# A quarter of the S5 turn tables moves from GpSimd to VectorE in a two-layer hybrid trunk

## The chip, the cores and the metric

The kernel runs as one program on one core of a Trainium2 chip. The metric is device microseconds for one execution. Engines are named as the profile names them: PE (TensorE), DVE (VectorE), ACT (ScalarE), POOL (GpSimd), and SP, whose queue issues most DMAs.

## The reference, cut to what matters

Two layers with the same structure work on 1024 tokens of width 1024 in fp32. Each layer normalises its input, projects it once, runs three branches on parts of the projection, and projects the concatenated result back:

```python
mod = silu(c) @ w_mod + b_mod                       # shift, scale, gate
h = rmsnorm(x, g_pre) * (1 + scale) + shift
a_q, a_k, a_v, a_g, b_q, b_k, b_v, b_lr, b_g, c_u, c_g = split(h @ w_in)
o_a = sliding_window_attention(a_q, a_k, a_v, sinks) * silu(a_g)
o_b = rmsnorm(gated_linear_attention(b_q, b_k, b_v, log_a), g_gla) * silu(b_g)
y = gelu(s5_ssm(c_u, a_re, a_im, log_dt, b_re, b_im, c_re, c_im, d))
o_c = y * sigmoid(y @ w_glu + b_glu) * silu(c_g)
x = x + gate * rmsnorm(concat(o_a, o_b, o_c) @ w_out, g_post)
```

The change lies in `s5_ssm`. It is a complex diagonal recurrence per state, h[t] = abar * h[t-1] + in[t], with abar = mag * (cos th + i sin th). The kernel takes 8 tokens as one step and turns the state's axes by the angle, so that the scan over 128 steps needs only the real factor rho = mag^8. For that it needs, for each of 32 groups of 64 states, the cosine and the sine of n times the angle of one step, for n from 0 to 127: the turn tables. They depend on the weights alone and are computed in the kernel, once per layer.

## The kernel before

**Stages of a layer.** The projection's products are split into a high and a low fp32r part: each weight tile is loaded by SP into `wraw` (3 buffers), cast by ACT to `whi` (L52) and subtracted on DVE to `wlo` (L53), 4 buffers each; PE then makes three matmuls for each product (L387 to L389, or L408 to L410 where the tokens are the output's rows). A queue of generators yields units of such projections, and other work is put between the units. A layer runs: the tail of the layer before; the values of the linear attention (`bv`, two projections) and its queries and keys (`bqk`, four) with the S5 tables between them; the linear attention (`gla`) with the S5 inputs (`cu`) and gates between; attention with the S5 scans between; the output projection.

**The table stage.** `s5_tables(l)` is a generator. It loads weights, forms `bf` and `cx`, and then runs two kinds of sub-generators for four parts q = 0 to 3: `blocks(q)`, which forms the tables E and O on DVE (`powmul`, L1179 to L1181), transposes E on PE into G and stores O and G to DRAM (L1170), and `turns(q)`, the turn tables. Part q starts two rounds after part q - 1. At the end come R (L1255, L1262) from the product `pk` of PE, and DMAs of R from SP (L1268, L1270). `gla_decay(l)` is put ahead of the rest of the tables after 10 units in layer 0, and after 18 in layer 1, where the tables have been issued in full by then. It transposes `lr` (L759, L760), multiplies (L768, L769, L770), takes Exp and Ln on ACT (L773, L774) and finishes the log decay on DVE (L778).

**The turn tables.** `turns(q)` works on 4 groups on each half of the partitions: tiles `cs` and `sn` of 128x4x128 and `rt` (a scratch), each with one buffer. It sets column 0 to 1 and 0 (L1217, L1218) and doubles the table seven times: with n = 1, 2, ..., 64 columns known, six products and sums of 128x4xn elements (L1225 to L1230) give the next n. Then the negated sine goes to the scratch (L1234), and three DMAs, issued from POOL's queue (L1235, L1237), store the sine's negative, the cosine and the sine to `s5turn` in DRAM. `s5_scan` reads them in the attention stage of the same layer (L1316), on SP's queue.

**After the stage.** `gla` clears `xq` on POOL (L694) and runs the scans `bc` on DVE (L786). POOL (L799), ACT (L800) and DVE (L804) then form the keys that PE transposes (L810).

**What sets the order.** The source is not the order on an engine. When the kernel is built, the framework sorts each engine's instructions by time estimates of its own: of those that it takes for ready, the one that stands earlier in the source goes first. A tile with one buffer is taken for ready when its last reader, a DMA included, is done by the estimate. On the chip each engine then works its list in order and waits on semaphores. (DVE's memset of `dc`, L1257, from the end of `s5_tables`, stands ahead of its first product, L1144, in the trace.)

Of the kernel before, what the change touches and what calls it, by code (L numbers as in the profile page):

```python
# [19 lines left out]
ALU = mybir.AluOpType  # L20
# [21 lines left out]
class Trunk:  # L42
# [1077 lines left out]
    def s5_tables(self, l):  # L1120
        nc = self.nc
        v, g_ = nc.vector, nc.gpsimd
# [88 lines left out]

        def turns(q):
            gs = slice(q * 4, q * 4 + 4)
            cs = st.tile([P, 4, P], F32, name="cs", bufs=1)
            sn = st.tile([P, 4, P], F32, name="sn", bufs=1)
            t3 = st.tile([P, 2, 4, 64], F32, name="rt", bufs=1)
            g_.memset(cs[:, :, 0:1], 1.0)  # L1217
            g_.memset(sn[:, :, 0:1], 0.0)  # L1218
            for k in range(7):
                n = 1 << k  # L1220
                zc = tcs[:, 0, k, gs].unsqueeze(2).to_broadcast([P, 4, n])
                zs = tcs[:, 1, k, gs].unsqueeze(2).to_broadcast([P, 4, n])
                a, b = t3[:, 0, :, 0:n], t3[:, 1, :, 0:n]
                lo, hi = slice(0, n), slice(n, 2 * n)
                g_.tensor_tensor(out=a, in0=sn[:, :, lo], in1=zs, op=ALU.mult)  # L1225
                g_.tensor_tensor(out=b, in0=cs[:, :, lo], in1=zs, op=ALU.mult)
                g_.tensor_tensor(out=cs[:, :, hi], in0=cs[:, :, lo], in1=zc, op=ALU.mult)
                g_.tensor_tensor(out=sn[:, :, hi], in0=sn[:, :, lo], in1=zc, op=ALU.mult)
                g_.tensor_tensor(out=cs[:, :, hi], in0=cs[:, :, hi], in1=a, op=ALU.subtract)
                g_.tensor_tensor(out=sn[:, :, hi], in0=sn[:, :, hi], in1=b, op=ALU.add)  # L1230
                if k > 3:
                    yield
            neg = t3.rearrange("p a g n -> p (a g n)").rearrange("p (g n) -> p g n", n=P)
            g_.tensor_scalar(out=neg, in0=sn, scalar1=-1.0, scalar2=1.0, op0=ALU.mult, op1=ALU.mult)  # L1234
            g_.dma_start(self.turn[l][:, 2, 4 * q:4 * q + 4, :], neg)  # L1235
            for slot, t in enumerate((cs, sn)):
                g_.dma_start(self.turn[l][:, slot, 4 * q:4 * q + 4, :], t)  # L1237

        flight = []
        for q in range(6):  # L1240
            if q < 4:
                flight.append(blocks(q))
                flight.append(turns(q))
            live = list(flight)
            for _ in range(2):
                for f in live:
                    if next(f, "end") != "end":
                        yield
                    elif f in flight:
                        flight.remove(f)  # L1250
        for f in flight:
# [9 lines left out]
                        in1=dc.unsqueeze(2).to_broadcast([P, 32, 16]), op=ALU.mult)  # L1261
# [352 lines left out]
```

## Time and profile before

| what | value |
|---|---|
| time, median of 3 runs | 1859.58 us (1851.38, 1859.58, 1863.3) |
| profiled execution | 1855.12 us, span 1853.3 us |
| PE busy | 1745.6 us (94% of the span) |
| DVE busy | 1342.5 us (72%) |
| ACT busy | 860.1 us (46%) |
| POOL busy | 586.2 us (32%) |
| mean granted PE clock | 0.979 of full speed |

The span runs from the first to the last instruction; the execution's own time lies 1.8 us above it. Busy shares are averages over stages with different limits; matmul ends are modelled, so a busy PE is not PE at its peak. Times in the rows below are microseconds from the span's start. A row's number in square brackets is the idle time of the engine just before it, with what ended it.

### The profile page before, as it was taken

The numbers are of one execution on the slowest core, as the hardware profiler recorded it, in microseconds if no ns is written. First come the engines' busy times: TensorE is split into PE (matmuls) and PEld (weight loads), VectorE is DVE, ScalarE is ACT, GpSimd is POOL, SyncE is SP. The second block draws the span as 40 slices with busy tenths as digits, with TensorE's granted clock in tenths as the row PEclk, the third lists the DMA queues.
The fourth block names the chain that finished last, engine by engine and source line by source line (L and its number), as shares of the span: only waits on it lengthen the run. The fifth ranks groups of instructions, "written<-read, shape, count | busy, mean of one in ns | idle before, by whom it ended". The sixth has DMA issues, their size and how long they took to land.

```text
span 1853.3 us, 28268 instructions
## 1 busy us (share of the span) xinstructions
PE 1745.6 (94%) x9403; PEld 1457.4 (79%) x9403; DVE 1342.5 (72%) x2975; ACT 860.1 (46%) x1973; POOL 586.2 (32%) x1005
## 2 busy tenths in 40 slices
PE   6999799999989989999998989999999899999998
PEld 5987588887777677788768968888888767878876
DVE  7876778479999788647675654974898978873534
ACT  5233333445556565446563243333555656642433
POOL 4269742212343354002116971411323511000100
PEclk8999899999999999999999999999999999999999
DMA  8144411235542322235464432212345111113342
GB/s 309 31 92 142 131 52 47 63 112 174 170 142 70 113 81 75 92 125 182 161 194 113 150 116 65 57 35 69 107 128 148 52 46 41 37 51 133 106 167 100
DMA packets 239385, 198.24 MB, mean 107 GB/s; under 512 B 49596, under 2 KB 195068, under 8 KB 239240
## 3 DMA queue, kind: packets, MB, share of 16 engines
q1 hardware_dynamic: 211640, 172.54, 31.0%
q10 hardware_dynamic: 25536, 16.80, 2.9%
q0 software_dynamic: 2064, 7.11, 1.0%
q8 instruction: 74, 1.21, 0.3%
q14 instruction: 71, 0.58, 0.1%
HBM read 163.13 MB, written 37.46 MB: 108 GB/s over the span
## 4 chain that ended last, share of the span: by engine, by line
PE 45%; DVE 9%; ACT 3%; issue 2%; DMA 2%; POOL 2%; ACTq 0%; DVEq 0%; POOLq 0%; SPq 0%
PE py L1486 15%; PE pj L387 5%; PE pj L389 5%; PE pj L388 5%; PE pj L1486 2%; PE pa L898 1%; PE pj L408 1%; PE pj L410 1%; PE pj L409 1%; DVE wlo L53 1%; PE pT L610 1%; PE pj L1384 1%; DVE pl L53 1%; DMA wraw<-in_w_out_dram 1%; DVE p L595 1%
## 5 line engine op out<-in xcount | busy, mean ns | idle before, releaser
L387 PE MATMUL pj<-H,whi 128*128 128x512 f32 x1088 | 442.8, 407 | 7.0 <-ACT M L665 3.2
L389 PE MATMUL pj<-H,wlo 128*128 128x512 f32 x1088 | 431.5, 397 | 3.2 <-DVE wlo L53 3.2
L388 PE MATMUL pj<-H,whi 128*128 128x512 f32 x1088 | 430.6, 396 | 0.0
L53 DVE TENSOR_TENSOR wlo<-wraw,whi 128x512 fp32r<-128x512 f32 (+1 forms) x320 | 237.1, 759 | 96.0 <-ACT whi L52 87.1
L52 ACT CAST whi<-wraw 128x512 fp32r<-128x512 f32 (+1 forms) x320 | 191.7, 618 | 179.2 <-PE pj L388 108.5
L387 PEld LDWEIGHTS pj<-H,whi 128*128 128x128 f32 x1088 | 207.4, 191 | 51.4 <-ACT M L665 3.6
L389 PEld LDWEIGHTS pj<-H,wlo 128*128 128x128 f32 x1088 | 206.6, 190 | 50.9 <-DVE wlo L53 4.2
L388 PEld LDWEIGHTS pj<-H,whi 128*128 128x128 f32 x1088 | 207.4, 191 | 39.9 <-issue 1.0
L600 ACT ACTIVATE p<-p,st 128x257 f32<-128x257 f32 (+1 forms) x256 | 125.7, 493 | 152.6 <-DVE st L595 138.7
L53 DVE TENSOR_TENSOR mlo<-M,mhi 128x384 fp32r<-128x384 f32 (+2 forms) x80 | 53.5, 676 | 141.6 <-ACT mhi L52 134.8
L1486 PE MATMUL py<-whi,mhi 128*128 128x512 f32 x448 | 142.6, 397 | 5.8 <-ACT mhi L52 3.1
L1486 PE MATMUL py<-wlo,mhi 128*128 128x512 f32 x448 | 145.1, 397 | 0.6 <-DVE wlo L53 0.5
L1486 PE MATMUL py<-whi,mlo 128*128 128x512 f32 x448 | 143.4, 394 | 0.7 <-DVE mlo L53 0.7
L1507 POOL TENSOR_SCALAR yrs<-yss 128x1 f32<-128x1 f32 x16 | 6.7, 418 | 376.0 <-ACT junk L1503 374.9
L52 ACT CAST mhi<-M 128x384 fp32r<-128x384 f32 (+2 forms) x80 | 50.3, 634 | 157.7 <-PE pj L1486 94.7
L595 DVE CUSTOM_DVE_ANT_0 p<-sc,bias,sink 128x256 f32<-128x256 f32 (+1 forms) x256 | 111.4, 462 | 5.7 <-PE sc L590 4.6
L1486 PEld LDWEIGHTS py<-whi,mhi 128*128 128x128 f32 x448 | 83.3, 188 | 27.6 <-ACT whi L52 5.3
L584 POOL COPY p<-sink 128x2 f32<-128x2 f32 x128 | 34.3, 270 | 221.2 <-PE pT L610 101.2
L1486 PEld LDWEIGHTS py<-wlo,mhi 128*128 128x128 f32 x448 | 84.4, 188 | 22.6 <-DVE wlo L53 3.7
L1486 PEld LDWEIGHTS py<-whi,mlo 128*128 128x128 f32 x448 | 84.4, 189 | 19.9 <-DVE mlo L53 1.5
L410 PE MATMUL pj<-wlo,H 128*128 128x256 f32 (+1 forms) x320 | 92.3, 291 | 6.2 <-DVE wlo L53 6.2
L408 PE MATMUL pj<-whi,H 128*128 128x256 f32 (+1 forms) x320 | 93.2, 292 | 3.8 <-DVE hv L346 2.7
(379 smaller groups left out, 3921.2 us busy)
## 6 DMA issues: line engine op xcount, KB each, us to landing
wraw<-in_w_in_dram SPq DMA_DIRECT2D x160, 256.0 KB
wraw<-in_w_out_dram SPq DMA_DIRECT2D x160, 256.0 KB
wraw<-in_w_mod_dram SPq DMA_DIRECT2D x64, 256.0 KB
M<-s5tab SPq DMA_DIRECT2D x32, 256.0 KB
M<-s5turn SPq DMA_DIRECT2D x64, 128.0 KB
M<-in_w_mod_dram SPq DMA_DIRECT2D x10, 512.0 KB
s5tab<-O ACTq DMA_DIRECT2D x8, 512.0 KB
s5tab<-G ACTq DMA_DIRECT2D x8, 512.0 KB
```

What stands on the lines that cost most here:

```text
L52: self.nc.scalar.copy(hi, src)
L53: self.nc.vector.tensor_tensor(out=lo, in0=src, in1=hi.bitcast(F32), op=ALU.subtract)
L387: nc.tensor.matmul(pj, hi, hh, start=(k == 0), stop=False)
L388: nc.tensor.matmul(pj, hi, hl, start=False, stop=False)
L389: nc.tensor.matmul(pj, lo, hh, start=False, stop=(k == KD - 1))
L408: nc.tensor.matmul(pj[:, :N], hh, hi, start=(k == 0), stop=False)
L409: nc.tensor.matmul(pj[:, :N], hl, hi, start=False, stop=False)
L410: nc.tensor.matmul(pj[:, :N], hh, lo, start=False, stop=(k == KD - 1))
L584: nc.gpsimd.tensor_copy(p[:, :, n], self.sink[:, h0:h0 + 2])
L595: nc.vector.tensor_tensor_reduce(out=p[:, h, 0:n], in0=sc[:, h * 256:h * 256 + n], in1=bias[:, h, o0:o0 + n], scale=-1.0, scalar=self.sink ...
L600: nc.scalar.activation(p[:, h, 0:n + 1], p[:, h, 0:n + 1], AF.Exp, bias=neg[:, h:h + 1], scale=-1.0, accum_out=den[:, h:h + 1])
L1486: self.nc.tensor.matmul(py[t, h], lhs, ws[h][w][:, 0, :], start=(n == 0 and first), stop=(n == N - 1 and last))
```

## The change

`turns(q)` takes its memsets, its 42 products and sums and the negation on DVE where q is 3, in both layers. The three DMAs stay on POOL's queue. The tiles and their single buffers are the same.

```diff
         def turns(q):
             gs = slice(q * 4, q * 4 + 4)
+            e_ = v if q == 3 else g_
             cs = st.tile([P, 4, P], F32, name="cs", bufs=1)
             sn = st.tile([P, 4, P], F32, name="sn", bufs=1)
             t3 = st.tile([P, 2, 4, 64], F32, name="rt", bufs=1)
-            g_.memset(cs[:, :, 0:1], 1.0)
-            g_.memset(sn[:, :, 0:1], 0.0)
+            e_.memset(cs[:, :, 0:1], 1.0)
+            e_.memset(sn[:, :, 0:1], 0.0)
             for k in range(7):
...
-                g_.tensor_tensor(out=a, in0=sn[:, :, lo], in1=zs, op=ALU.mult)
...
+                e_.tensor_tensor(out=a, in0=sn[:, :, lo], in1=zs, op=ALU.mult)
...
-            g_.tensor_scalar(out=neg, in0=sn, scalar1=-1.0, scalar2=1.0, op0=ALU.mult, op1=ALU.mult)
+            e_.tensor_scalar(out=neg, in0=sn, scalar1=-1.0, scalar2=1.0, op0=ALU.mult, op1=ALU.mult)
             g_.dma_start(self.turn[l][:, 2, 4 * q:4 * q + 4, :], neg)
```

The other five products and sums of a step change in the same way.

## Rows read from the trace of the kernel before

**Rows 1.** Waits, 198 to 220 us: waiter, awaited, us in total, times, longest.
```profile
PE pk L810 <- DVE M L804: 11.7, 1, 11.7
```

**Rows 2.** Waits, 1083 to 1100 us.
```profile
PE pj L387 <- ACT M L665: 3.2, 1, 3.2
```

**Rows 3.** Timeline of DVE in layer 0: start, us, instruction.
```profile
199.24 8.19 DVE L53 TENSOR_TENSOR wlo<-wraw,whi 128x512 fp32r<-128x512 f32 x2 [7.39 <-ACT whi L52]
207.36 6.80 DVE L786 TENSOR_TENSOR_SCAN bc<-ones,M 128x128 f32<-128x128 f32 x16
```

**Rows 4.** Timeline of DVE in layer 1.
```profile
1045.21 1.52 DVE L1181 TENSOR_TENSOR O<-O,pm_t 128x1024 f32<-128x1024 f32 x1
1056.58 0.69 DVE L1255 COPY R<-pk 128x512 f32<-128x512 f32 x1 [9.85 <-PE pk L1198]
...
1060.77 2.31 DVE L53 TENSOR_TENSOR wlo<-wraw,whi 128x512 fp32r<-128x512 f32 x3 [2.73 <-ACT whi L52]
1065.57 1.28 DVE L760 COPY M<-plr 16x512 f32<-16x512 f32 x2 [2.49 <-PE plr L759]
...
1083.03 5.82 DVE L778 SCALAR_TENSOR_TENSOR M<-M 128x512 f32<-128x512 f32 x1 [5.70 <-ACT M L774]
...
1091.76 6.80 DVE L786 TENSOR_TENSOR_SCAN bc<-ones,M 128x128 f32<-128x128 f32 x16
```

**Rows 5.** Timeline of POOL in layer 0.
```profile
194.32 0.20 POOL L1225 TENSOR_TENSOR rt<-sn,tcs 128x4 f32<-128x4 f32 x1 [1.28 <-DMA s5turn<-rt]
...
207.42 0.54 POOL L1235 DMA_DIRECT2D s5turn<-rt  x1
```

**Rows 6.** Timeline of POOL in layer 1.
```profile
986.56 0.10 POOL L1217 MEMSET cs<- 128x4 f32 x1 [7.86 <-PE pj L339]
...
1010.89 9.07 POOL L1226 TENSOR_TENSOR rt<-cs,tcs 128x16 f32<-128x16 f32 x1
...
1052.55 0.10 POOL L1217 MEMSET cs<- 128x4 f32 x1 [2.27 <-DMA s5turn<-cs]
...
1072.56 0.10 POOL L1217 MEMSET cs<- 128x4 f32 x1 [2.10 <-DMA s5turn<-cs]
...
1075.49 0.70 POOL L1225 TENSOR_TENSOR rt<-sn,tcs 128x4 f32<-128x4 f32 x1 [0.79 <-DMA s5turn<-rt]
...
1087.55 0.76 POOL L1230 TENSOR_TENSOR sn<-sn,rt 128x256 f32<-128x256 f32 x1
```

**Rows 7.** Timeline of ACT in layer 0.
```profile
201.35 0.62 ACT L52 CAST whi<-wraw 128x512 fp32r<-128x512 f32 x1 [2.14 <-PE pj L388]
```

**Rows 8.** DVE: timeline at 105 us; then a group by shape (count, busy, mean ns).
```profile
105.73 0.22 DVE L1086 TENSOR_TENSOR pa__1200<-M 128x64 f32<-128x64 f32 x1
105.88 0.22 DVE L1087 TENSOR_TENSOR pb__1201<-M 128x64 f32<-128x64 f32 x1
...
L1331 DVE TENSOR_TENSOR s5a<-s5a 128x256 f32<-128x256 f32 x32 | 13.4, 418 | 4.7 <-POOL s5a L1330 3.8
```

**Rows 9.** Timelines of ACT and POOL in one gelu step of layer 1.
```profile
1466.58 0.60 ACT L52 CAST whi<-wraw 128x512 fp32r<-128x512 f32 x1
...
1467.96 0.59 ACT L473 ACTIVATE qs<-pj 64x512 fp32r<-64x512 f32 x1
1469.34 0.63 ACT L1365 ACTIVATE ge<-ge 128x512 f32<-128x512 f32 x1 [0.79 <-POOL ge L1364]
...
1467.52 1.78 POOL L1364 TENSOR_TENSOR ge<-ge,M 128x512 f32<-128x512 f32 x1
```

**Rows 10.** Timeline of PE in layer 1.
```profile
1062.62 0.39 PE L389 MATMUL pj<-H,wlo 128*128 128x512 f32 x1
...
1068.66 0.69 PE L768 MATMUL pz<-M,wa 16*128 16x512 f32 x1
```

**Rows 11.** View of the tile rt: its DMAs from issue to landing.
```profile
DMA to landing us min/median/max: 2.5/4.3/5.5
```

**Rows 12.** Windows in layer 0: length, busy us by engine, PE clock, DMA share, GB/s.
```profile
218.00:222.00 4.00, 3.84 (x13) 3.43 (x14) 3.96 (x3) 2.25 (x4) 4.00 (x3) 0.50 0.02 5
```

More of the change, by code (lines that the diff above doesn't have):

```diff
@@ L1224, in turns @@
                 lo, hi = slice(0, n), slice(n, 2 * n)
-                g_.tensor_tensor(out=a, in0=sn[:, :, lo], in1=zs, op=ALU.mult)
[L1226 to L1230, printed above, removed]
+                e_.tensor_tensor(out=a, in0=sn[:, :, lo], in1=zs, op=ALU.mult)
+                e_.tensor_tensor(out=b, in0=cs[:, :, lo], in1=zs, op=ALU.mult)
+                e_.tensor_tensor(out=cs[:, :, hi], in0=cs[:, :, lo], in1=zc, op=ALU.mult)
+                e_.tensor_tensor(out=sn[:, :, hi], in0=sn[:, :, lo], in1=zc, op=ALU.mult)
+                e_.tensor_tensor(out=cs[:, :, hi], in0=cs[:, :, hi], in1=a, op=ALU.subtract)
+                e_.tensor_tensor(out=sn[:, :, hi], in0=sn[:, :, hi], in1=b, op=ALU.add)
                 if k > 3:
```

## The prediction

> **What bounds the kernel now.** I read the page's first part, then the waits of TensorE (PE), then the timelines of VectorE (DVE) and GpSimd (POOL) over the two stages in which the turn tables are made. PE is busy nearly all the time, so an edit on DVE or POOL is worth only what PE waits for it. In layer 0 PE makes no matmul for 11.7 us before L810, whose input comes from DVE L804 [rows 1]; in layer 1 it stands 3.2 us for a PSUM tile that ACT L665 frees late [rows 2]. Both waits end a chain that starts with the scans bc (L786).
>
> In layer 0 bc starts at 207.36, behind two weight splits (L53) that took 8.19 us together [rows 3]; R, an operation of the same width, takes 0.69, so two of them should take 1.4 [rows 4]. The same microsecond is the end of POOL's turn tables: their last DMA issue is at 207.42 [rows 5]. In layer 1 one L778 took 5.82 us, until 1088.85 [rows 4]; POOL's last table product starts at 1087.55 and lasts 0.76 [rows 6]. So DVE stood still while POOL ran products back to back. It goes the other way too: one POOL product of 128x16 elements took 9.07 us [rows 6] while DVE worked without a gap. The reader should keep both: POOL's last table holds up DVE on the chain that PE waits for, and DVE makes POOL's second table late.
>
> **The part that leaves POOL.** Per layer POOL loses 2 memsets, 42 products and the negation. Its own time is no term: the tables are read only in the attention stage. The credit is the end of DVE's stall. Layer 0: the second split's input comes at 201.97 [rows 7], so bc could start at 202.6 instead of 207.36, 4.8 us earlier. Layer 1: 5.82 less 0.7 is 5.1 us on the chain to L665, of which PE can use its wait of 3.2.
>
> At this credit the rows and the notes differ. L778 waited through nine POOL products, none over 0.76 us long near its end [rows 4, 6]. The Trainium skill (SBUF — State Buffer, section "SBUF: two separate sides") says that a DVE instruction with two SBUF inputs and a GpSimd one that reads SBUF take turns under an exclusive lock, held for the whole of one instruction. Read as a wait for one instruction, that gives L778 a credit of 0.8 us at most, and the sum below would end about 2 us higher. The trace shows the loser waiting for many, so I keep 5.1.
>
> **The part that DVE gains.** 45 instructions per layer. The 30 products up to 128x64 and the two memsets: DVE starts one of 128x64 0.15 us after the one before and is busy 0.22 [rows 8], so 32 of them take 4.8 to 7.0 us. Six of 128x128, between 0.22 and 0.42, take 1.3 to 2.5; six of 128x256 at 0.42 take 2.5 [rows 8]; the negation 0.7, as R [rows 4]. Sum 9.3 to 12.7 us; I take 9.5, since successive instructions overlap in the rows. It would be hidden where DVE is idle: 9.9 us before R at 1056.58, and 5.7 before L778 [rows 4].
>
> **The wait that the change adds.** cs, sn and rt have one buffer each. DVE's first memset must therefore wait until POOL has finished the third table and its DMAs have landed. In layer 1 POOL itself waited for them until 1072.56 (cs) and 1075.49 (rt) [rows 6]. DVE works in order, so everything queued behind that memset waits too. What is queued there is decided when the kernel is built: among the instructions that it takes for ready, the planner picks the one earlier in the source. The trace of before can't show where it puts the new ones, but it shows how it reckons POOL. In the gelu step it gave ACT four other instructions, from 1466.58 to 1468.55, between the square and the tanh, and then let the tanh wait 0.79 us for POOL's two operations [rows 9]. So it charges POOL about what POOL needs undisturbed, or less, and no stall. Undisturbed, the third table took 17.9 us: from 1052.55 to 1072.56, less the wait of 2.10 [rows 6]. Starting at 986.56 [rows 6], three of them end at about 1041, and the planner has the buffers free at about 1043. On the chip DVE slowed the second table, and the buffers come 30 us later. By the planner's reckoning the fourth table thus fits into DVE's idle stretch between the last O (ends 1046.4) and R (1056.58) [rows 4], and I expect it there in the order.
>
> **What that costs in layer 1.** Behind the table stand R, its sum, and the three splits of 1060.77 [rows 4], which give the weights of the first projection after the values. PE uses their lower halves from 1062.62 on [rows 10], so nothing covers a delay. The late end of the wait is 1075.5. The early end: POOL loses less to R, the splits and L760 (some 1.8 us, an estimate), and the landing of rt takes 2.5 us, the shortest, instead of 5.5, the longest [rows 11]: 1070.7. Half a microsecond of the table goes ahead of rt, 9.0 us follow: it ends between 1079.7 and 1084.5. R and its sum (1.4) and a split (0.7) come next, so PE gets its weights between 1081.8 and 1086.6, 19.2 to 24.0 us late. I take 19.2, the early end, because SP's loads stand behind R's DMAs and the queues are then quiet. After 11.7 us without work PE ran at half the clock in layer 0 (0.50 of full speed, the lower of the levels 1.2 and 2.4 GHz, from 218 to 222 [rows 12]); those 4 us hold work for 2, so I add 2 us. Against it, the chain to L665 moves by 21.2 less 5.1, and PE by 21.2, so PE no longer waits the 3.2. Layer 1: 19.2 + 2 - 3.2 = +18. Who else waits: R's eight DMAs on SP, with three weight loads behind them, wanted a projection later (some 11 us of PE's work hides them; without that they cost about 5), and the table's three DMA issues on POOL, now waiting for DVE, with the clearing of xq and L799 behind them. Those aren't wanted before bc, so they cost nothing; with DVE later than bc they would add their own 2 us each.
>
> **Layer 0.** The same wait would run to 194.3, when rt is free [rows 5], and the table to about 203. Splits stand further ahead of PE there, and a late one costs it between nothing and 12 us (203 against about 191, when the projection then due has used up its first half; an estimate). PE would meet its wait at L810 that much later, and that wait shrinks by up to 5. So the ends are -4.8 (bc at 202.6) and +7. I take 0, near the middle, as no row is nearer to either.
>
> **Sum.** The profiled execution took 1855.1 us, 1.8 beyond its span, and 4.5 below the median of the three runs (1859.6, from 1851.4 to 1863.3). With +18 and 0 it would take 1873; from the median, which I forecast, 1878. A change under 1% (18.6 us) can hardly be told from none in this kernel, and the forecast stands at that border.
>
> **Rivals.** A, not slower: the planner charges POOL 25 us or more per table. Then it has the buffers free only after about 1063; the table stands behind the splits and most of the decay (L760, L770) and runs in the gaps from 1072.6 on; L778 loses its stall, PE its wait. Layer 0 gives -3 (the table ends near 204, bc follows), layer 1 -3.2: 1853. For it: what holds up L778 and layer 0's bc is just the work that leaves. Against it: the gelu rows. It decides at the point where the memset stands behind L760 in DVE's order. B, between: the table stands behind the splits but ahead of L760 (1065.57 [rows 4]) or L770. PE then waits at L768 (1068.66 [rows 10]), which needs L760's output, for up to 16 us, or for some 6 if only L770 is late: +4 to +16, 1870 in the middle. C, earlier: the planner charges less than 17.9, and the table stands ahead of the last O and E (O's product starts at 1045.21 [rows 4]), so that the transposes of block 3 wait too, some 10 us of PE's work earlier (an estimate): +28, 1888. In any of them the new order may also move work elsewhere. That the change doesn't do what it says is excluded by the diff.
>
> **How the numbers follow.** Forecast 0.48, A 0.25, B 0.14, C 0.13. The forecast's own range, by the bounds of layer 1 (18.0 to 22.8, 3 more if the table takes 12.7) and of layer 0, is 1871 to 1889. The range 1853 to 1889 takes in A's and B's times; it leaves out half of A and half of C, some 2 in 10. Slower by over 1% is nearly half of the forecast, most of C and a little of B: 0.40. Faster by over 1% would need 18.6 us, beyond A's two credits together (8.0 at most), so only a new order elsewhere could give it: 0.03. Within 1%: 0.57.
>
> **What would show it.** Right: in layer 1 DVE's 45 new instructions stand between O and R, with an idle stretch of 20 us or more before them, ended by a DMA of s5turn; PE waits 19 us or more at L389 for a split near 1062; L778 takes 0.7 us; PE has no wait at L665. Wrong: L760 ahead of the table in DVE's order, or a wait of only a few microseconds at the memset. The sum is wrong too if the planner's new order moves more elsewhere than in these two stages.

## The result, and the profile after

The changed kernel takes 1911.1 us (median of four, 1907.27 to 1913.27) where the kernel before takes 1857.25: 1.0291 times as long [1.0266 to 1.0316], 54 us more. The prediction was 1878, with a range that ended at 1889. The profiled execution took 1913.21 us, its span 1911.4, which is 58.1 above that of before. The lines of `turns` and behind it stand one further down than before.

The page's first part, busy time by engine:

```profile
PE 1758.2 (92%) x9403; PEld 1466.4 (77%) x9403; DVE 1332.4 (70%) x3065; ACT 859.4 (45%) x1973; POOL 531.9 (28%) x915
```

DVE has its 90 instructions more, POOL 90 fewer. PE makes the same 9403 matmuls in 12.6 us more. Part of that is not the change's. Up to the first product of the table stage (L1144), ahead of every changed instruction, before and after (length, busy us by engine, granted clock of PE, DMA share, GB/s):

```profile
0.00:115.76 115.76, 95.82 (x647) 88.59 (x648) 87.22 (x340) 42.52 (x84) 38.05 (x84) 0.88 0.49 155
0.00:119.22 119.22, 100.56 (x647) 93.24 (x648) 87.49 (x341) 42.52 (x84) 38.10 (x84) 0.84 0.47 151
```

The same 647 matmuls took 4.7 us more at a lower granted clock, and the stage starts 3.5 us later. In nine other profiles below the same matmuls took from 91.8 (0.92) to 97.5 us (0.87). Less these 3.5 us the profiled pair differs by 54.6, as the medians do (54).

The rest are waits. PE's waits, from 140 to 240 us (layer 0):

```profile
PE pz L768 <- DVE M L760: 32.6, 1, 32.6
```

and from 1040 to 1130 us (layer 1):

```profile
PE pj L408 <- ACT whi L52: 21.7, 1, 21.7
PE pj L410 <- DVE wlo L53: 2.3, 1, 2.3
```

Neither of the two large ones is in the rows of before. The two that were [rows 1, 2] shrank: L810 waits 6.9 us instead of 11.7, and L665 holds up PE no more. DVE's timeline shows what both new waits stand behind. Layer 0:

```profile
148.52 1.21 DVE L1180 TENSOR_TENSOR pm_t<-pw,bf 128x1024 f32<-128x1024 f32 x1
181.35 0.06 DVE L1218 MEMSET cs<- 128x4 f32 x1 [31.61 <-DMA s5turn<-cs]
182.49 1.23 DVE L1181 TENSOR_TENSOR E<-E,pm_t 128x1024 f32<-128x1024 f32 x1 [1.08 <-DMA s5turn<-sn]
...
190.05 1.27 DVE L760 COPY M<-plr 16x512 f32<-16x512 f32 x2
...
206.43 0.43 DVE L1235 TENSOR_SCALAR rt<-sn 128x512 f32<-128x512 f32 x1
208.38 2.50 DVE L778 SCALAR_TENSOR_TENSOR M<-M 128x512 f32<-128x512 f32 x4 [1.53 <-ACT M L774]
```

Layer 1, the rows that answer to [rows 4]:

```profile
1060.05 1.31 DVE L1180 TENSOR_TENSOR pm_t<-pw,cx 128x1024 f32<-128x1024 f32 x1
1086.59 0.06 DVE L1218 MEMSET cs<- 128x4 f32 x1 [25.24 <-DMA s5turn<-cs]
1088.14 1.23 DVE L1181 TENSOR_TENSOR O<-O,pm_t 128x1024 f32<-128x1024 f32 x1 [1.49 <-DMA s5turn<-sn]
...
1117.10 0.69 DVE L1256 COPY R<-pk 128x512 f32<-128x512 f32 x1 [6.25 <-PE pk L1198]
...
1143.56 0.69 DVE L778 SCALAR_TENSOR_TENSOR M<-M 128x512 f32<-128x512 f32 x1 [5.69 <-ACT M L774]
```

In both layers the first memset of the moved table stands in the midst of the block products, between a product `pm_t` and the sum that uses it, and DVE does nothing for 31.6 and 25.2 us until a transfer of POOL's third table has landed. Behind it wait, in layer 0, the last two blocks and L760, whose input PE had finished at 155.4; in layer 1 the second block's O and the last two blocks. L778 takes 0.69 us instead of 5.82.

In layer 1 PE's wait is put down to ACT, which had no work of its own then. ACT's timeline (ACTq is its sequencer, which issues DMAs):

```profile
1061.79 0.59 ACT L1202 COPY G<-pg 128x512 f32<-128x512 f32 x1 [0.52 <-PE pg L1197]
1089.40 0.37 ACTq L1170 DMA_DIRECT2D s5tab<-O  x1
1089.81 0.37 ACT L676 COPY M<-pj 128x256 f32<-128x256 f32 x1 [27.44 <-DVE rt L1227]
1090.08 0.18 ACT L678 COPY lr<-pj 128x16 f32<-128x16 f32 x1
1090.14 1.67 ACT L52 CAST whi<-wraw 128x512 fp32r<-128x512 f32 x3
```

The store of O is issued from ACT's queue. O was complete at 1089.37 (1088.14 and 1.23), the issue followed at 1089.40, and the casts that PE needed stood behind it. (The releaser named in the third row, L1227, is a product that ran just then; nothing of ACT's depends on it.)

POOL's timeline, the third table of each layer from its first memset to its first transfer:

```profile
165.66 0.11 POOL L1218 MEMSET cs<- 128x4 f32 x1
...
178.88 0.59 POOL L1238 DMA_DIRECT2D s5turn<-cs  x1
...
1070.80 0.10 POOL L1218 MEMSET cs<- 128x4 f32 x1
...
1084.07 0.59 POOL L1238 DMA_DIRECT2D s5turn<-cs  x1
```

DVE stood still beside both, so this is a table undisturbed: 13.2 and 13.3 us to the first transfer, of which some 1.2 us are waits for transfers of the table before, and 15.7 and 15.8 until the memset of the next owner could start.

The clock, in windows of layer 0 and layer 1 just behind the waits (length, busy us by engine, granted clock, DMA share, GB/s):

```profile
190.00:200.00 10.00, 9.22 (x17) 5.24 (x18) 7.47 (x29) 1.79 (x3) 0.00 (x0) 0.53 0.23 73
...
1091.00:1100.00 9.00, 6.75 (x41) 6.46 (x42) 9.00 (x12) 2.27 (x6) 0.00 (x0) 0.66 0.64 203
```

**Sum for the profiled pair.** PE's waits: L768 +32.3, L408 +21.7, L810 -4.8, L665 -3.2, which is 46.0; all rows of PE's waits over the whole span sum to 99.4 us before and 145.3 after, 45.9 more. PE's own busy time: +12.6. Together 58.6, against 58.1 measured.

### The profile page after: what moved, and what is told of

Read it like the earlier page. It is cut to its first block, busy times and chain, and to the rows that moved or that the text cites. A ratio compares the mean times of both kernels' runs of the same rounds, so it can differ in the third digit from the quotient of the medians.

```text
span 1911.4 us, 28269 instructions
## 1 busy us (share of the span) xinstructions
PE 1758.2 (92%) x9403; PEld 1466.4 (77%) x9403; DVE 1332.4 (70%) x3065; ACT 859.4 (45%) x1973; POOL 531.9 (28%) x915
## 4 chain that ended last, share of the span: by engine, by line
PE 41%; DVE 9%; POOL 4%; ACT 3%; DMA 3%; issue 2%; ACTq 0%; DVEq 0%; SPq 0%; POOLq 0%
PE py L1487 14%; PE pj L387 5%; PE pj L389 5%; PE pj L388 5%; PE pj L1487 2%; DMA wraw<-in_w_out_dram 1%; PE pa L898 1%; DVE wlo L53 1%; DVE p L595 1%; PE pj L1385 1%; DVE pl L53 1%; PE pT L610 1%; DVE p L604 1%; POOL cs L1230 1%; PE po L621 1%
## 5 line engine op out<-in xcount | busy, mean ns | idle before, releaser
L387 PE MATMUL pj<-H,whi 128*128 128x512 f32 x1088 | 444.6, 409 | 3.4 <-ACT ut L1278 1.4
L53 DVE TENSOR_TENSOR wlo<-wraw,whi 128x512 fp32r<-128x512 f32 (+1 forms) x320 | 224.0, 718 | 104.0 <-ACT whi L52 95.5
L387 PEld LDWEIGHTS pj<-H,whi 128*128 128x128 f32 x1088 | 208.1, 191 | 48.6 <-issue 3.9
L52 ACT CAST mhi<-M 128x384 fp32r<-128x384 f32 (+2 forms) x80 | 50.3, 634 | 157.0 <-PE pj L1487 92.6
L408 PE MATMUL pj<-whi,H 128*128 128x256 f32 (+1 forms) x320 | 94.4, 296 | 25.4 <-ACT whi L52 22.7
```

Source lines behind the costliest of these rows:

```text
L52: self.nc.scalar.copy(hi, src)
L53: self.nc.vector.tensor_tensor(out=lo, in0=src, in1=hi.bitcast(F32), op=ALU.subtract)
L387: nc.tensor.matmul(pj, hi, hh, start=(k == 0), stop=False)
L408: nc.tensor.matmul(pj[:, :N], hh, hi, start=(k == 0), stop=False)
```

## The experiments

**Theory.** The loss is DVE standing at the memset, in order, for buffers that POOL still uses; its price is the wait's length, less what covers the instructions queued behind it. **Rivals.** The work itself (45 instructions a layer among the block products); a new order elsewhere; and, for the size, one layer or both.

**1. Buffers of its own** (`own_tiles`). `cs` and `sn` of the fourth part take over the buffers of two tiles that are done by then (`tw` leaves the set that it shared, which goes from five buffers to four); its scratch is new. The diff is shortened.

```diff
-            cs = st.tile([P, 4, P], F32, name="cs", bufs=1)
+            cs = st.tile([P, 4, P], F32, name="cs", tag="tw" if q == 3 else "cs", bufs=1)
...
+            sn = ... tag="cin" if q == 3 else "sn"
+            t3 = ... tag="rt3" if q == 3 else "rt"
```

> The fourth table stays on VectorE in both layers, with the same 45 instructions, but cs, sn and the scratch have buffers of their own for it (two of them take over tiles that are done by then), so that its first memset waits for no transfer of GpSimd's third table. Theory, the queued wait: nearly all of the 54 us come from VectorE standing at that memset with the block products, the splits and the decay behind it; then this kernel takes 1848 to 1862 us (the time before, less up to 8 us for the stalls that GpSimd's fourth table caused), and VectorE shows no idle time ended by an s5turn transfer. Rival, the work: the 45 instructions themselves, 9 us a layer among the block products, make the products late and PE waits for them; then it stays above 1880. Rival, a new order: the planner's other choices cost the time; then it also stays above 1880, since the table stands amid the products here too.

Measured: 1851.39 us, 0.9961 times the time before [0.9934 to 0.9988]. DVE's timeline:

```profile
128.14 1.21 DVE L1181 TENSOR_TENSOR O<-O,pm_t 128x1024 f32<-128x1024 f32 x1
129.30 0.06 DVE L1218 MEMSET cs<- 128x4 f32 x1
129.31 0.06 DVE L1219 MEMSET sn<- 128x4 f32 x1
```

The table stands even earlier among the block products, with all its instructions, and no idle time before it; in layer 1 too. The whole loss is gone, and with it both rivals of work and order.

**2. One layer at a time** (`only_l0`, `only_l1`): `e_ = v if q == 3 and l == 0 else g_`, and the same with `l == 1`.

> The changed kernel with the edit in layer 0 alone. Theory, the queued wait in both layers: by the idle time before the memset and PE's waits behind it layer 0 costs 27 to 33 us of the 54: 1884 to 1891 us. Rival, the prediction's own step: layer 0 costs nothing and layer 1 all: 1852 to 1862.

> The changed kernel with the edit in layer 1 alone. Theory, the queued wait in both layers: 21 to 27 us of the 54, 1878 to 1885 us, and with the kernel that has it in layer 0 alone the two costs add up to the whole change within 5 us. Rival: layer 1 costs all, 1905 or more.

Measured: 1883.5 us, ratio 1.0148 [1.0090 to 1.0206], with a memset wait of 31.5 us and 32.1 at L768; and 1883.19, ratio 1.0135 [1.0092 to 1.0177], with 25.7 and 21.9 at L408. The two add up to 1.0283, the whole change is 1.0291. By the medians each layer costs about 26 us, though four runs each leave it uncertain by 8 to 11; the rival, by which layer 0 costs nothing, is the prediction's and it falls.

**3. Another part** (`first_part`, `second_part`, `third_part`): `e_ = v if q == 0 else g_`, and 1 or 2 in place of 0. The same work on DVE, the single buffers kept, and none, one or two tables of POOL's ahead of it.

> The first part of the tables is on VectorE in place of the fourth, with the single buffers of the change. VectorE's memset then stands ahead of all block products and has no earlier table to wait for; instead GpSimd's first table of its own, the second part, waits for VectorE's transfers, at the start of the stage. Theory, the queued wait: 1848 to 1866 us, within 1% of the time before, and POOL's tables end earlier than before. Rival, the work: the same 45 instructions ahead of the block products cost as much as behind them, above 1880.

> The second part is on VectorE in place of the fourth, with the single buffers. Its memset waits for GpSimd's first table alone and stands ahead of the block products' first sum. Theory, the price is the wait of the queue: about 10 us in layer 0, where VectorE has slowed the first table until then, and 0 to 3 in layer 1, where the first table ran undisturbed: 1860 to 1873 us. Rival, the price is the same for any part that follows another engine's table: 1900 or more.

> The third part is on VectorE in place of the fourth, with the single buffers. Its memset waits for GpSimd's first two tables. In VectorE's order it stands behind the first O in layer 0 and ahead of it in layer 1, earlier than the fourth part's, because the planner has two tables ready by then. Theory, the price is the wait of the queue: with VectorE still, GpSimd needs some 16 us for the second table, so the waits should be about 25 us in layer 0 and 10 to 14 in layer 1 (31.6 and 25.2 with the fourth part), and the price about as many: 1884 to 1897 us. Rival: the price is the block products' and the decay's late start by the table's own work, the same for any part: 1905 or more.

| part on DVE | wait at its memset, layers 0 and 1 | time | ratio |
|---|---|---|---|
| first | none, none | 1855.03 | 0.9994 [0.9969 to 1.0019] |
| second | 6.4, none | 1856.84 | 1.0007 [0.9990 to 1.0025] |
| third | 21.8, 11.3 | 1882.67 | 1.0149 [1.0126 to 1.0173] |
| fourth (the change) | 31.6, 25.2 | 1911.1 | 1.0291 [1.0266 to 1.0316] |

DVE and PE's waits with the third part:

```profile
152.81 0.06 DVE L1218 MEMSET cs<- 128x4 f32 x1 [21.82 <-DMA s5turn<-cs]
...
1043.59 0.06 DVE L1218 MEMSET cs<- 128x4 f32 x1 [11.30 <-issue]
```

```profile
PE pg L1197 <- DVE E L1181: 19.3, 1, 19.3
...
PE pg L1197 <- DVE E L1181: 8.2, 1, 8.2
```

("issue" stands where the profile names no releaser; the memset of `sn` just behind waits for a DMA of s5turn.) Waits of 33.1 us in all cost 27.6 (1.49% of 1854.5), waits of 56.8 cost 54, and none cost nothing that can be told. With the third part PE waits 27.5 us in the two places, and 4.8 and 3.2 less at L810 and L665; over the span its waits sum to 21.5 us more than before, and its busy time is 5.6 longer. The time lies just below what I expected. With the second part DVE does wait in layer 0; the profile shows the idle time at the instruction that starts together with the memset:

```profile
126.37 0.69 DVE L1148 TENSOR_TENSOR tw<-bx,pw 128x512 f32<-128x512 f32 x1 [6.42 <-DMA s5turn<-cs]
126.37 0.06 DVE L1218 MEMSET cs<- 128x4 f32 x1
```

```profile
PE pj L408 <- ACT M L676: 5.7, 1, 5.7
```

PE meets nearly all of it, since ACT's L676 stands behind a copy (L1161) that waited for DVE's L1160. But L810 waits 7.0 us instead of 11.7 and L665 holds up PE for 1.4 instead of 3.2, 6.5 less together, so that the time is that of before. I had expected a wait of about 10 us and 1860 us or more: the wait was shorter, and I had left the credits out.

**4. The place in the queue** (`behind_R`, `behind_decay`). The two memsets become operations that give the same constants from R, or from the last output of the decay, so that the table can't stand ahead of it.

```diff
+                for t, c in ((cs, 1.0), (sn, 0.0)):
+                    v.tensor_scalar(out=t[:, :, 0:1], in0=R[:, 0:4, 0:1], scalar1=0.0, scalar2=c,
+                                    op0=ALU.mult, op1=ALU.add)
```

> The fourth table on VectorE with the single buffers, but its two memsets are replaced by operations that read R and give the same constants, so that the table can't stand ahead of R in VectorE's order. In layer 1 it then stands between R with its sum and the splits, with the decay behind it: the place that the prediction named. In layer 0 it stands behind the decay and R, ahead of the scans. Theory, the place in the queue sets the price: layer 1 costs what the prediction worked out for this place, 18 us (up to 23), and layer 0 some 0 to 9 us, since the table's own 9 us stand ahead of the scans, less the 5 us of the stall: 1875 to 1889 us. Rival: the place matters little and the price is the wait's length alone, wherever it stands: 1900 or more.

> As the one behind R, but the two first operations read the last output of the log decay, so that the table stands behind the decay and ahead of the scans in both layers. GpSimd's third table is then stored, and VectorE has no long wait left. Theory, the place in the queue sets the price: only the table's own 9 us stand ahead of the scans, and the stalls of 5 us in each layer are gone: 1855 to 1868 us, and the wait at the first operation is 5 us at most. Rival, the price is the wait wherever it stands: 1880 or more.

Measured behind R: 1869.81 us, ratio 1.0069 [1.0044 to 1.0094], 13 us more than before and less than I expected. In layer 1 the table stands just where the prediction put it, behind R and ahead of the splits. DVE, and PE's one wait beside it (1050 to 1110 us):

```profile
1055.20 0.69 DVE L1269 TENSOR_TENSOR R<-R,dd 128x512 f32<-128x512 f32 x1
1069.41 0.17 DVE L1220 TENSOR_SCALAR cs<-R 128x4 f32<-128x4 f32 x1 [13.52 <-DMA s5turn<-cs]
...
1077.35 1.30 DVE L53 TENSOR_TENSOR wlo<-wraw,whi 128x512 fp32r<-128x512 f32 x2
```

```profile
PE pj L389 <- DVE wlo L53: 14.6, 1, 14.6
```

So PE waits at the line that I named, 14.6 us where I had 19.2 or more. In layer 0 the wait at L810 falls to 5.1, and L768 waits 2.2. Over the span PE's waits sum to 12.0 us more than before, and its busy time is 5.1 longer.

Measured behind the decay: 1870.69 us, ratio 1.0073 [1.0045 to 1.0101]; 1855 to 1868 was expected, a small miss. In layer 0 DVE still waits there, 15.1 us where I expected 5 at most, and PE then waits 7.8 at L387 for ACT's L665. In layer 1 there is no wait, but POOL's third table now falls on the splits:

```profile
1065.32 7.94 DVE L53 TENSOR_TENSOR wlo<-wraw,whi 128x512 fp32r<-128x512 f32 x3 [5.61 <-ACT whi L52]
...
1097.55 0.17 DVE L1220 TENSOR_SCALAR cs<-M 128x4 f32<-128x4 f32 x1
...
1104.77 6.80 DVE L786 TENSOR_TENSOR_SCAN bc<-ones,M 128x128 f32<-128x128 f32 x16
```

The table itself, which ran here without other work between, took 7.2 us (1097.55 to 1104.77). Over the span PE's waits sum to only 6.2 us more than before; 8.4 more are PE's busy time, so that this run can't tell the price of the place well.

**5. What POOL's fourth table costs** (`no_fourth`): `turns(3)` ends at once, and part 2's tiles are stored twice. A quarter of the tables is left out.

> No engine computes the fourth part: the third part's tables are stored a second time in its place, so that the attention stage reads the same bytes. It leaves out a quarter of the turn tables and measures what GpSimd's fourth table costs. The prediction's credit was 3 to 5 us in layer 0 and 3.2 in layer 1: 1849 to 1852 us. Rival: the stalls that it causes are hidden or come back as other waits, within 2 us of the time before. Where the kernel with buffers of its own on VectorE is as fast as this one, VectorE's 90 instructions cost nothing there.

Measured: 1857.45 us, ratio 0.9997 [0.9981 to 1.0014]: no gain, as the rival said. DVE and PE's waits in layer 1:

```profile
1058.37 7.94 DVE L53 TENSOR_TENSOR wlo<-wraw,whi 128x512 fp32r<-128x512 f32 x3 [5.61 <-ACT whi L52]
...
1087.39 0.69 DVE L778 SCALAR_TENSOR_TENSOR M<-M 128x512 f32<-128x512 f32 x1 [5.69 <-ACT M L774]
```

```profile
PE pj L389 <- DVE wlo L53: 5.7, 2, 4.2
```

L778's stall is gone, and so is PE's wait at L665, but the stall has moved to three splits, which take 7.94 us instead of 2.31 [rows 4] while POOL's now last table ends; PE waits 4.2 us more for them. Layer 0 shows L810 at 5.1 instead of 11.7. These waits sum to -5.6 us. The profiled execution has 8.1 us more PE busy time for the same matmuls, which undoes them; the profiled executions of kernels with the same matmuls differ by up to 12 us in that (1742.2 with buffers of its own, 1754.0 behind the decay). Of the 8.1 us, 1.4 lie ahead of the table stage (97.2 us against 95.8); the rest I haven't followed.

**6. Buffers alone, and more on DVE** (`own_pool`, `alt_pool`, `alt_dve`). The first has experiment 1's tiles with `e_ = g_`. The other two use the second set for `q % 2`, with `e_ = g_` or `e_ = v if q % 2 else g_`.

> All four tables on GpSimd, the fourth with buffers of its own. It tells what the second set of buffers does without VectorE: GpSimd no longer waits 1 to 2 us for transfers before the fourth table, and no table leaves it. If the gain of the kernel with buffers of its own on VectorE comes from the work that leaves GpSimd, this takes the time before within 0.3% (1852 to 1863 us); if it comes from the buffers, it is as fast as that one, 1851 or less.

> All four tables on GpSimd, with two sets of buffers taken in turn, so that no table waits for the transfers of the one before it. The kernel with a set for the fourth part alone gained 7 us with all the work on GpSimd; if the gain comes from GpSimd's waits for transfers (2 us each, three per layer), this one gains as much or a little more: 1847 to 1853 us. If it came from the place that the planner gave the fourth table, this is within 0.3% of the time before.

> The second and the fourth table on VectorE in the second set of buffers, the first and the third on GpSimd in the first set: twice the work that the change moves. VectorE's fourth table waits for transfers of its own second table, which the planner reckons as the chip runs them. Theory, only the queued wait on the other engine's table costs: 1847 to 1858 us, although VectorE does 180 instructions more in all. Rival, VectorE's work has a price that begins with the second table: 1865 or more.

Measured: 1850.7 us, ratio 0.9962 [0.9946 to 0.9978]; 1853.39, ratio 0.9973 [0.9958 to 0.9988]; 1857.72, ratio 0.9999 [0.9987 to 1.0012]. All four tables on POOL with a second set are as fast as with the fourth on DVE (0.9961), so the gain of 7 us comes with the buffers and not with the move. Twice the work on DVE takes the time before, but it is 4.3 us slower than its like with all work on POOL (1857.72 against 1853.39; the two intervals meet only at 0.9987 and 0.9988), and over the span PE's waits sum to 99.4 us against 92.6. So the doubled move isn't free. DVE waits once more in it; its timeline, and the issue on POOL that it waits for:

```profile
161.30 1.21 DVE L1181 TENSOR_TENSOR E<-E,pm_t 128x1024 f32<-128x1024 f32 x1
176.09 0.06 DVE L1218 MEMSET cs<- 128x4 f32 x1 [13.58 <-DMA s5turn<-cs]
...
172.38 0.54 POOL L1238 DMA_DIRECT2D s5turn<-cs  x1
```

The buffer that this memset takes over is that of DVE's own second table, which was complete at 152.1 us. But its transfers are issued from POOL's queue, and there they stand behind POOL's third table. I had expected no such wait. By then the decay's products (L770) and all blocks but the last O are done. Between 120 and 215 us PE's only wait that the kernel before doesn't have is one of 3.8 us for ACT's L665; whether it comes from the 13.6 isn't followed. A wait of the same kind and nearly the same length (13.5) cost 14.6 us of PE's time behind R in layer 1.

## Why the prediction was wrong

**The mechanism held.** The added wait is what I said it was: the memset behind POOL's third table, ended by a DMA of s5turn (31.6 and 25.2 us), everything behind it in DVE's order late, PE idle, the clock down behind it (0.53 and 0.66). Without the shared buffers the loss is 0 (experiment 1). The direction was right; the size was not, and the place was not. 54 us were measured where the sum had +18, and the place is at the root of both parts of the error, about 26 us in layer 0 and about 8 in layer 1.

**The step that failed: "undisturbed, the third table took 17.9 us", as the planner's charge.** From it I had the buffers free at 1043 by the planner's reckoning, behind the last O. The built order shows less. The rows of before, DVE, at which the new memset stands (the third part's ahead of the first and the third row, the fourth part's ahead of the second and the fourth):

```profile
136.08 1.52 DVE L1181 TENSOR_TENSOR E<-E,pm_t 128x1024 f32<-128x1024 f32 x1
...
146.43 1.23 DVE L1181 TENSOR_TENSOR E<-E,pm_t 128x1024 f32<-128x1024 f32 x1
...
1018.68 1.21 DVE L1181 TENSOR_TENSOR O<-O,pm_t 128x1024 f32<-128x1024 f32 x1
...
1026.96 1.23 DVE L1181 TENSOR_TENSOR O<-O,pm_t 128x1024 f32<-128x1024 f32 x1
```

One table more moves the place by about 12 us in layer 0 (the third part's memset stands one product ahead of its row, at 134.8) and by 8.3 in layer 1; from the second part to the third it is 12.5 and 11.4. And three tables fit into 40.4 us from the first memset in layer 1 (986.56 [rows 6] to 1026.96), 13.5 each at most. So the planner charges some 8 to 13 us a table (an estimate from these places; its own figures aren't in any trace), where the chip needs 15.7 with DVE still and more beside it. The place is shown; that a low charge for POOL puts it there is argued. I set the planner's time for POOL beside the chip's times for DVE, here as in the prediction, and what the planner charges DVE moves the place as well; no run changes either charge. I had read this from the gelu step [rows 9], "about what POOL needs undisturbed, or less", and then took the upper end for a number; and the 17.9 was itself not undisturbed. The consequence was rival C, which had 0.13: the table ahead of the last O and E. Its price, 28 us for layer 1 with layer 0 at nothing, is close to what layer 1 cost, about 26, but partly by luck: rival C had PE wait for the transposes of block 3, and it waited for casts behind O's store on ACT.

**The second, and the larger in us: layer 0 at nothing.** It cost about 26 us. I had only asked how late the splits and bc would be. The table stood ahead of L760 there, because gla_decay runs amid the tables in layer 0, and nothing covers L760: PE waited 32.6 us for it. The bounds, -4.8 to +7, left this place out.

**The price at the place that I named was nearer.** There (experiment 4, behind R) PE waits 14.6 us against 19.2: the buffers were free at 1069.4 and the table took 7 us, where I had 1070.7 to 1075.5 and 9.0. With my own terms, +18 in layer 1 and the credit of 4.8 in layer 0, the sum would have been 13, and 0.69% of 1858, which is 13, was measured. That the two agree is partly luck: the wait is 4.6 us shorter than my term, and PE's busy time is 5.1 longer. The forecast's own range also had a slip: its bounds give 1873 to 1889 (1892 with the longer table) where I wrote 1871 to 1889. The measured time is outside either.

**Smaller terms.** DVE's 45 instructions: 9.5 taken from 9.3 to 12.7, measured 7.2 with nothing between them, below my lower end; in the changed kernel the products of 128x4 to 128x32 mostly start 0.07 to 0.12 us apart, where I had 0.15 from one row. The credits: bc's stall in layer 0 (L810 4.8 us shorter) and L778's (0.69, and no wait at L665) came as worked out in the changed kernel; but they belong to a particular meeting of POOL's table and DVE's work. When POOL's work simply ends a table earlier, the stall goes to the splits. Rival A took such a credit for the whole answer, and experiment 5 gives 0 for it.

**The weighed rule.** Three splits that take 7.94 us beside POOL products of 0.42 to 0.74 us show the same as L778 did before: DVE lost many turns in a row. The Trainium skill (SBUF — State Buffer, section "SBUF: two separate sides") has the lock held for the whole of one instruction; read as taking turns one by one, that gives three splits 2.2 us at most, and not these 5.6. No run here shows how the turns are given.

**ACT** was not in my list of who waits. O's store is issued from its queue, so that a late O stopped ACT for 27.4 us, and through it the casts for PE.

**What stays open:** why the second set of buffers gains 7 us on POOL. In the profile of `alt_pool` (1851.15 us) L810 waits 6.9 us instead of 11.7 and PE waits for L665 no more, and over the span PE's waits sum to 92.6 us against 99.4. So the gain looks like the end of the stalls that I had credited to the move. The profile of `own_pool` can't settle it: it took 1858.61 us, the longest of its twelve executions, with 9.6 us at L810. How the second set keeps POOL's tables from meeting DVE's work there is not followed.

## What to carry to other kernels

When an operation goes to an engine that works in order, and its tile has one buffer that another engine wrote before, look in the built order where its first instruction stands, and list all that is queued behind it and the DMA issues on other queues that need it: the price is the wait less their cover, and was anything from 0 to 32 us of PE's time in a layer here for the same 7 us of work. The planner's opinion of the engines sets that place; where the chip is slower than the opinion, the first instruction waits, and here it waited longer with each table ahead. Give the moved operation buffers of its own first, taken from tiles that are done: here that removed all of the loss, and the buffers alone gained about what the move had been credited with. See also whose queue issues the stores: with two tables on DVE, DVE waited 13.6 us for a store of its own table that stood in POOL's queue.

## What the runs showed of the hardware

- POOL and DVE hold each other up through many instructions, in either direction and wherever they meet: three splits 7.94 us instead of 2.31, one L778 5.82 instead of 0.69. Taking one table from POOL moved the meeting to other instructions and did not end it.
- The two memsets and 42 products of a table take 13.2 us on POOL with DVE still, 1.2 us of waits for transfers included; on DVE they take 7.2 us together with the negation (two constant operations in place of the memsets).
- A store whose tile isn't complete holds up the compute instructions behind it on the issuing engine: ACT stood still for 27.4 us for O.
- After a wait of 32.6 us PE ran at 0.53 of full speed for the next 10 us (near the lower of the levels 1.2 and 2.4 GHz), and after 21.7 us at 0.66 for 9.
- The same 647 matmuls at the start of the program took from 91.8 to 100.6 us of PE's busy time in eleven profiled executions, at a granted clock from 0.92 to 0.84. Two profiles can differ by as much before any instruction that was changed.
